# Block sums of weights formed by accumulating transfers instead of VectorE subtractions

## The chip, the cores and the metric

The kernel runs on one core of a Trainium2 chip. Time is device time in microseconds (us) of one execution; the number that counts is the median of several executions. The engines are TensorE (PE for its matmuls, PEld for its weight loads), VectorE (DVE), ScalarE (ACT), GpSimd (POOL) and SyncE (SP). SP issues nearly all transfers between HBM and the on-chip memory (SBUF); POOL can issue transfers too, on a queue of its own, and such a transfer may add what it reads to what already stands at its destination. Matrix products gather in PSUM, which ACT and DVE read.

## The reference

A trunk of two layers, float32, with 512 tokens and a model width of 1024. Each layer is a feed-forward network (FFN), a token mixing of three branches, and a second FFN, each between two norms:

```python
def _swiglu(t, w_gate, w_up, w_down):
    return (jax.nn.silu(t @ w_gate) * (t @ w_up)) @ w_down

for l in range(2):
    f = _swiglu(_rmsnorm(h, ffn1_pre_g[l]), ffn1_w_gate[l], ffn1_w_up[l], ffn1_w_down[l])
    h = h + 0.5 * _rmsnorm(f, ffn1_post_g[l])
    ...            # projections, stick-breaking, forgetting and memory attention, gates, w_out
    f = _swiglu(_rmsnorm(h, ffn2_pre_g[l]), ffn2_w_gate[l], ffn2_w_up[l], ffn2_w_down[l])
    h = h + 0.5 * _rmsnorm(f, ffn2_post_g[l])
```

`w_gate` and `w_up` are 1024 x 2816 each: 22 feature tiles of 128 columns. The change is about the products `t @ w_gate` and `t @ w_up` of twelve of these tiles in each of the four FFNs.

## The kernel before

**Matrix products in three passes.** Every float32 operand is split into a high half, rounded to a shorter format by ACT (L188), and a low half, the difference, by DVE (L189). `mm3` (L212 to L216) then makes three matmuls: high by high, high by low, low by high. A tile of weights is thus loaded (SP), split (ACT, then DVE), and read by PE. The names of the trace follow this: `raw_...` is a loaded tile, `wh_...` and `wl_...` its halves. `us_...` and `ag...` are halves of activations.

**Queue of weights.** Work on weights is a list of jobs (class `Queue`, L372). A job names its units (128x1024 tiles of weights, 512 KB). Ahead of a job, `load_ahead` splits the units of the jobs that come (at least 4 units), and `fetch_ahead` issues their transfers as far as buffers allow. Rings of buffers: two for "raw", four each for "wh" and "wl", six for "v". A scheduler puts the instructions of each engine in an order when the program is built, by estimated times; on the chip each engine works through its own list in that order, and waits where an operand or a buffer isn't there yet.

**Token-major groups.** In each FFN (named a and c for the first and second of a layer; trace names such as `kta`, `pta` or `ktc` leave the numbers out) the feature tiles 14, 16, 18, 20 and 0 are plain pairs, and three groups at f = 2, 6 and 10 (`TG`, L637) cover twelve tiles. A group takes a 2x2 block product, tokens by features, with gate and up side by side, and computes it with seven block products instead of eight, in the order n = 0, 2, 3, 4, 5, 1, 6 (`ORDER`, L640). The weights of a group are four blocks: B00 and B10, the upper and lower half of the rows of `w_gate`, and B01 and B11, the same of `w_up`; each block is two tiles, k0 = 0 and k0 = 2. So a product is a job of two units with 12 matmuls each. The right-hand operand of each product:

| n | weights | formed from |
|---|---|---|
| 0 | B00 | loaded |
| 2 | B01 - B00 | kept, `t` |
| 3 | B11 - B01 + B00 | kept, `t` |
| 4 | B11 | loaded |
| 5 | B11 - B01 | kept, `b` |
| 1 | B10 | loaded |
| 6 | B10 minus the operand of n = 3 | kept, `t` |

The signs of the activation sums (`sums`, L693, on DVE) go with them. `BlockUnit.load` (L328) forms the sums with one DVE subtraction each: L337 for n = 2, L340 for n = 3, L345 for n = 5, L349 for n = 6. They are written in place into two kept tiles per k0, which are of the ring "v" (six buffers, four used by a group). B00 and B10 are loaded a second time for n = 2 and n = 6, B01 and B11 once: 14 loads by SP for a group (L313). After a product, PSUM goes to SBUF by ACT (copies L741, silu L739, L745) or DVE (additions L743); `feature_major` (L751) turns the result.

**What lies around the groups.** The first FFN starts with loads of the input, norms, constants (POOL makes two masks with L144 and L150 in `more_constants`, L139) and small vectors by POOL transfers (`vectors`, L121, turned by PE at L127). In the first group of that FFN stand the statistics of the input `mem` (`mem_stats`, L1057 to L1069): its two 128x1024 tiles (`mst`) are taken from the ring "v" too, ACT squares them (L1062) and changes its function table for Ln and Exp (L1064). At the start of each later FFN, the norm of the four token tiles (L592 to L631: residual and square L601 and L602, normed L608, transposed on PE L618, halves by ACT and DVE) runs beside the last product of the stage before and the first loads of the new weights; `park` (L777) stores the hidden state.

Of the kernel before, what the change touches and what calls it, by code (L numbers as in the profile page):

```python
# [9 lines left out]
F32 = mybir.dt.float32  # L10
F32R = mybir.dt.float32r
BF16 = mybir.dt.bfloat16
AF = mybir.ActivationFunctionType
ALU = mybir.AluOpType
# [3 lines left out]
P = 128  # L18
# [4 lines left out]
def kernel(  # L23
# [38 lines left out]
    nc = tc.nc  # L62
    _, S, D = x.shape
# [3 lines left out]
    ND = D // P  # L67
# [37 lines left out]
    def stile(shape, tag, name, dt=F32R):  # L105
        return sb.tile(shape, dt, tag=tag, bufs=BUFS[tag], name=name)
# [134 lines left out]
    class Unit:  # L241


        def __init__(self, src, k0, nk, c0, ncol, name, scale=None):
            self.tags, self.place = ("wh", "wl"), "raw"
            self.src, self.k0, self.nk, self.c0, self.ncol, self.name, self.scale = src, k0, nk, c0, ncol, name, scale
            self.h = self.raw = None
# [9 lines left out]
        def fetch(self):  # L257
            if not self.waits():
                return
            Q.fetched += self.ring()  # L260
            self.raw = stile([P, self.nk, self.ncol], self.place, "raw_" + self.name, F32)
            nc.sync.dma_start(self.raw[:], self.src[self.k0 * P:(self.k0 + self.nk) * P, self.c0:self.c0 + self.ncol]
                              .rearrange("(k p) c -> p k c", p=P))

        def load(self):
            if self.h is not None:
                return
            self.fetch()
            self.split_from(self.raw[:])
            self.loaded()  # L270
# [17 lines left out]
    class BlockUnit(Unit):  # L288
# [7 lines left out]
        BLOCKS = ((0, 0), (1, 0), (0, 0), None, None, (0, 1), (1, 0))  # L296
# [31 lines left out]
        def load(self):  # L328
            if self.h is not None:
                return  # L330
            self.fetch()
            t = self.keep.get(0, self.k0) if self.n >= 2 else None
            b = self.keep.get(1, self.k0) if self.n >= 3 else None
            if self.n < 2:
                src = self.raw[:]
            elif self.n == 2:
                nc.vector.tensor_tensor(t, t, self.raw[:], ALU.subtract)  # L337
                src = t
            elif self.n == 3:
                nc.vector.tensor_tensor(t, b, t, ALU.subtract)  # L340
                src = t
            elif self.n == 4:
                src = b
            elif self.n == 5:
                nc.vector.tensor_tensor(b, b, self.raw[:], ALU.subtract)  # L345
                src = b
            else:
                ins = (t, self.raw[:]) if self.pair is None else (self.raw[:], t)
                nc.vector.tensor_tensor(t, *ins, ALU.subtract)  # L349
                src = t  # L350
            self.split_from(src)
            if self.ring():
                self.raw = None
                Q.fetched -= 1
            Q.fetch_ahead()
# [125 lines left out]
    Q = Queue()  # L481
# [160 lines left out]
    def ffn(l, src, wg, wu, wd, dst, name, spare, aside=None):  # L642
# [78 lines left out]
        def gate_up(f, n, uns):  # L721
            if n in (0, 1, 2):
                st["gb", SUM[n]] = [pbank("mm", f"pt{name}_{f}_{n}_{e}") for e in range(2)]
            pts = st["gb", SUM[n]]
            opens, ends = n in (0, 1, 2), n in (1, 4, 6)
            for un in uns:
                for k in range(un.nk):
                    kk = un.k0 + k
                    for e in range(2):
                        mm3(pts[e][:], *input_block(n, kk, e), un.h[:, k], un.l[:, k], opens and kk == 0,  # L730
                            ends and kk == ND // 2 - 1, free=True)
                        yield 3 * S * PE_US
            i, j = TO[n]
            if n in (0, 2, 3, 6):
                st["c", i, j] = stile([P, 2, S], "f", f"c{name}_{f}_{i}{j}", F32)
            t = st["c", i, j]
            for e in range(2):
                if n == 6:
                    nc.scalar.activation(t[:, e], pts[e][:], AF.Silu)  # L739
                elif n in (0, 2, 3):  # L740
                    nc.scalar.copy(t[:, e], pts[e][:])  # L741
                else:
                    nc.vector.tensor_tensor(t[:, e], t[:, e], pts[e][:], ALU.add)  # L743
            if n == 1:
                nc.scalar.activation(t[:], t[:], AF.Silu)  # L745
            if n in (1, 6):
                u = st["c", i, 1]
                nc.vector.tensor_tensor(u[:], u[:], t[:], ALU.mult)
                st["hid", f, i] = u

        def feature_major(f):  # L751

            for i in range(2):
                u = st.pop(("hid", f, i))
                for b in range(2):
                    f2 = f + 2 * b
                    pt = pbank("z", f"th{name}_{f2}_{i}")
                    for m in range(2):
                        for e in range(2):
                            nc.tensor.transpose(pt[:, (2 * m + e) * P:(2 * m + e + 1) * P],  # L760
                                                u[:, e, (2 * b + m) * P:(2 * b + m + 1) * P], ident[:])
                    yield 0.45
                    out_ = pt[:].rearrange("p (m q) -> p m q", m=2)
                    nc.scalar.copy(pair(f2)[:, :, HALVES[i]], out_)

        def group(f):

            keep = Keep(lambda i, k0: stile([P, 2, S], "v", f"kt{name}_{f}_{i}_{k0}", F32)[:])
            for n in ORDER:
                uns = []  # L770
                for k in range(0, ND // 2, 2):
                    uns.append(BlockUnit(n, wg[l], ND // 2, k, 2, S, keep, f"t{name}_{f}_{n}_{k}", (wg[l], wu[l])))
                    uns[-1].c0 = f * P
                yield uns, (lambda n=n, uns=uns: gate_up(f, n, uns))
            yield [], lambda: feature_major(f)
# [140 lines left out]
        def turns(f):  # L916
            *jobs, turn = group(f)
            later.append(turn)
            return iter(jobs)
# [774 lines left out]
    for l in LAYERS:  # L1694
        i, mn = 3 * l, []
# [42 lines left out]
```

## Time and profile before

| | |
|---|---|
| median of 3 runs | 2389.71 us (2389.67 to 2389.91) |
| the profiled execution | 2390.63 us, with a span of 2388.9 us |
| busy in the span | PE 2377.2, PEld 2010.7, DVE 1842.9, ACT 1320.8, POOL 74.2 us |
| granted TensorE clock | 0.999 |
| transfers | 334.00 MB, mean 140 GB/s |

The span runs from the first to the last instruction of the profiled execution. Its rows give, for a group of instructions: line, engine, operation, output and inputs with sizes, the count, then busy time, the mean in ns of one, and the idle time just before them with what ended it. A row of the timeline gives the start, the length, the engine and the line; matmuls are pipelined, so their lengths overlap. The view of stretches gives busy us of PE, PEld, DVE, ACT and POOL between two times, then the granted clock, the busy share of the 16 DMA engines, and GB/s. The rows of transfers give the median time from issue to landing.

### The profile page before, as it was taken

Reading aid. Unit: us, or ns where it says so; the run is one execution under the profiler, and the core shown is the slowest. Engines: PE = TensorE matmul, PEld = TensorE weight load, DVE = VectorE, ACT = ScalarE, POOL = GpSimd, SP = SyncE. Lnnn points to the kernel's source line nnn. Section 1 sums busy time; section 2 is a strip of 40 time slices with the busy share of each in tenths; the row PEclk is TensorE's granted clock in tenths of the full one; section 3 lists DMA queues with packets and bytes.
Section 4 is the critical chain, followed back from the end, with each engine's and each line's share of the span. In section 5 each row is a group of like instructions: output and inputs, shape, how many; then the busy total and the mean of one; then the engine's idle time right before and its main releaser. Section 6 shows DMA issues by size and latency. Waiting matters only on the chain.

```text
span 2388.9 us, 30985 instructions
## 1 busy us (share of the span) xinstructions
PE 2377.2 (100%) x11736; PEld 2010.7 (84%) x11736; DVE 1842.9 (77%) x2535; ACT 1320.8 (55%) x2144; POOL 74.2 (3%) x130
## 2 busy tenths in 40 slices
PE   9999999999999999999999999999999999999998
PEld 8888888888888898888898888888888888988887
DVE  7786887677876687769787878876787766778686
ACT  5655455576655555554545554656675655455543
POOL 0000000001110000000000000000001100000000
PEclk9999999999999999999999999999999999999999
DMA  5554554222223445545545546532232244445453
GB/s 188 165 174 136 202 183 143 71 76 77 88 62 116 158 135 174 169 148 195 184 141 166 178 140 220 174 109 80 63 98 71 71 141 142 159 143 183 141 198 129
DMA packets 233979, 334.00 MB, mean 140 GB/s; under 512 B 10315, under 2 KB 133475, under 8 KB 233829
## 3 DMA queue, kind: packets, MB, share of 16 engines
q1 hardware_dynamic: 233728, 331.98, 42.8%
q8 instruction: 92, 1.51, 0.3%
q14 instruction: 59, 0.48, 0.1%
q0 software_dynamic: 96, 0.03, 0.0%
q10 hardware_dynamic: 4, 0.00, 0.0%
HBM read 319.39 MB, written 12.58 MB: 139 GB/s over the span
## 4 chain that ended last, share of the span: by engine, by line
PE 95%; DVE 3%; ACT 1%; DMA 1%; issue 0%; DVEq 0%; ACTq 0%
PE pg L216 3%; PE pg L214 3%; PE pg L215 3%; PE pta L214 3%; PE ptc L216 3%; PE pta L216 3%; PE ptc L215 3%; PE pta L215 3%; PE ptc L214 3%; PE pda L214 3%; PE pda L215 3%; PE pda L216 3%; PE pdc L216 3%; PE pdc L215 3%; PE pdc L214 3%; PE pb L214 2%
## 5 line engine op out<-in xcount | busy, mean ns | idle before, releaser
L214 PE MATMUL pg<-us_a,wh_wg 128*128 128x512 f32 x384 | 150.6, 392 | 0.0
L216 PE MATMUL pg<-us_a,wl_wg 128*128 128x512 f32 x384 | 149.6, 390 | 0.0
L215 PE MATMUL pg<-us_a,wh_wg 128*128 128x512 f32 x384 | 149.5, 389 | 0.0
L188 ACT CAST wh_tc<-ktc 128x1024 fp32r<-128x1024 f32 x60 | 62.6, 1052 | 83.3 <-DVE ktc L349 32.4
L188 ACT CAST wh_ta<-kta 128x1024 fp32r<-128x1024 f32 x60 | 62.6, 1053 | 80.2 <-DVE kta L349 34.1
L189 DVE TENSOR_TENSOR wl_tc<-ktc,wh_tc 128x1024 fp32r<-128x1024 f32 x60 | 72.8, 1223 | 24.4 <-ACT wh_tc L188 24.2
L189 DVE TENSOR_TENSOR wl_ta<-kta,wh_ta 128x1024 fp32r<-128x1024 f32 x60 | 72.9, 1223 | 23.4 <-ACT wh_ta L188 22.9
L216 PE MATMUL pdc<-wh_dc,alc 128*128 128x512 f32 x224 | 87.3, 390 | 0.3 <-DVE alc L189 0.3
L215 PE MATMUL pdc<-wl_dc,ahc 128*128 128x512 f32 x224 | 87.2, 389 | 0.0
L214 PE MATMUL pdc<-wh_dc,ahc 128*128 128x512 f32 x224 | 87.1, 389 | 0.0
L214 PE MATMUL pda<-wh_da,aha 128*128 128x512 f32 x224 | 87.1, 389 | 0.0
L215 PE MATMUL pda<-wl_da,aha 128*128 128x512 f32 x224 | 87.1, 389 | 0.0
L216 PE MATMUL pda<-wh_da,ala 128*128 128x512 f32 x224 | 87.1, 389 | 0.0
L192 DVE SCALAR_TENSOR_TENSOR wl_wg<-raw_wg,wh_wg 128x1024 fp32r<-128x1024 f32 x48 | 58.8, 1224 | 34.0 <-ACT wh_wg L191 29.5
L216 PEld LDWEIGHTS pg<-us_a,wl_wg 128*128 128x128 f32 x384 | 72.1, 188 | 15.2
L215 PEld LDWEIGHTS pg<-us_a,wh_wg 128*128 128x128 f32 x384 | 72.2, 188 | 14.3
L214 PEld LDWEIGHTS pg<-us_a,wh_wg 128*128 128x128 f32 x384 | 72.1, 188 | 14.3
L214 PE MATMUL pta<-wh_ta,aga 128*128 128x512 f32 x192 | 75.2, 391 | 0.0
L214 PE MATMUL ptc<-wh_tc,agc 128*128 128x512 f32 x192 | 75.0, 391 | 0.0
L216 PE MATMUL pta<-wh_ta,aga 128*128 128x512 f32 x192 | 74.7, 389 | 0.0
L216 PE MATMUL ptc<-wh_tc,agc 128*128 128x512 f32 x192 | 74.7, 389 | 0.0
L215 PE MATMUL ptc<-wl_tc,agc 128*128 128x512 f32 x192 | 74.7, 389 | 0.0
(536 smaller groups left out, 7691.3 us busy)
## 6 DMA issues: line engine op xcount, KB each, us to landing
raw_da<-in_ffn_w_down_dram SPq DMA_DIRECT2D x58, 512.0 KB, 3.6
raw_dc<-in_ffn_w_down_dram SPq DMA_DIRECT2D x58, 512.0 KB, 3.4
raw_ta<-in_ffn_w_gate_dram SPq DMA_DIRECT2D x48, 512.0 KB, 3.7
raw_wg<-in_w_gate_dram SPq DMA_DIRECT2D x48, 512.0 KB, 3.5
raw_tc<-in_ffn_w_gate_dram SPq DMA_DIRECT2D x48, 512.0 KB, 3.6
kta<-in_ffn_w_up_dram SPq DMA_DIRECT2D x24, 512.0 KB, 4.9
raw_wo<-in_w_out_dram SPq DMA_DIRECT2D x24, 512.0 KB, 3.3
ktc<-in_ffn_w_up_dram SPq DMA_DIRECT2D x24, 512.0 KB, 5.7
```

The lines of the kernel that those rows point to most:

```text
L188: both = [nc.scalar.copy(h_ap, src)]
L189: make = lambda: nc.vector.tensor_tensor(l_ap, src, h_ap.bitcast(F32), ALU.subtract)
L192: make = lambda: nc.vector.scalar_tensor_tensor(l_ap, src, scale, h_ap.bitcast(F32), ALU.mult, ALU.subtract)
L214: nc.tensor.matmul(pt, lh, rh, start=start, stop=False, skip_group_check=free)
L215: nc.tensor.matmul(pt, lh, rl, start=False, stop=False, skip_group_check=free)
L216: nc.tensor.matmul(pt, ll, rh, start=False, stop=stop, skip_group_check=free)
```

## The change

A new class `SumUnit` takes the place of `BlockUnit` in the groups. It keeps three tiles per k0, so a group holds all six buffers of the ring "v". No sum is formed on DVE any more: ACT writes the negative of a tile into a kept buffer, and a transfer issued by POOL adds another block to it. That block comes from HBM, or in one case from another kept buffer:

| at the load of | before it in the buffer | ACT writes | POOL's transfer adds | then used by |
|---|---|---|---|---|
| n = 0 | | buf0 = -B00 | B01 from HBM | n = 2 |
| n = 0 | buf1: B01, loaded | buf1 = -B01 | B11 from HBM | n = 5 |
| n = 2 | buf2: B00, loaded | | buf1 from SBUF | n = 3 |
| n = 3 | | buf0 = -buf2 | B10 from HBM | n = 6 |

Every row holds for both k0. In a group SP issues 10 loads instead of 14 (three raw blocks and the first contents of buf1 and buf2, each for both k0), POOL issues 8 accumulating transfers, ACT writes 6 negations, and 8 DVE subtractions go. The loads of buf1 and buf2 are issued together with the raw block of n = 0. The order of the products, the matmuls and the splits stay. The new lines move everything behind them down by 71 lines.

```diff
+    class SumUnit(BlockUnit):
+        BLOCKS = ((0, 0), (1, 0), None, None, (1, 1), None, None)
+        def __init__(self, n, src, rows, k0, nk, ncol, keep, name, pair=None, three=True):
+            super().__init__(n, src, rows, k0, nk, ncol, keep, name, pair)
+            self.kept = {2: 0, 3: 2 if three else 1, 5: 1, 6: 0}.get(n)
+            self.three = three
...
+        def plus(self, i, b):
+            if isinstance(b, int):
+                src = self.buf(b)
+            else:
...
+            nc.gpsimd.dma_start(self.buf(i), src, accum_op=ALU.add)
+        def minus(self, i, src):
+            nc.scalar.activation(self.buf(i), src, AF.Copy, scale=-1.0)
+        def fetch(self):
...
+            if self.n == 0:
+                self.block(self.buf(1), (0, 1))
+                if self.three:
+                    self.block(self.buf(2), (0, 0))
+        def load(self):
...
+            self.split_from(self.raw[:] if self.kept is None else self.buf(self.kept))
+            if self.n == 0:
+                self.minus(0, self.raw[:])
+                self.plus(0, (0, 1))
+                self.minus(1, self.buf(1))
+                self.plus(1, (1, 1))
+            elif self.n == 2:
+                if self.three:
+                    self.plus(2, 1)
...
+            elif self.n == 3:
+                self.minus(0, self.buf(self.kept))
+                self.plus(0, (1, 0))
...
-                    uns.append(BlockUnit(n, wg[l], ND // 2, k, 2, S, keep, f"t{name}_{f}_{n}_{k}", (wg[l], wu[l])))
+                    uns.append(SumUnit(n, wg[l], ND // 2, k, 2, S, keep, f"t{name}_{f}_{n}_{k}", (wg[l], wu[l])))
```

`three` is true wherever the class is used; its other branch, with two kept tiles, isn't reached.

More of the change, by code (lines that the diff above doesn't have):

```diff
@@ L351, in load, with buf @@
             self.split_from(src)
+            if self.ring():
+                self.raw = None
+                Q.fetched -= 1
+            Q.fetch_ahead()
+    class SumUnit(BlockUnit):
[4 more added lines that the diff above has]
+            self.three = three
+        def buf(self, i):
+            return self.keep.get(i, self.k0)
+        def plus(self, i, b):
+            if isinstance(b, int):
+                src = self.buf(b)
+            else:
+                r = (b[0] * self.rows + self.k0) * P
+                src, c = (self.src, b[1] * self.ncol) if self.pair is None else (self.pair[b[1]], self.c0)
+                src = src[r:r + self.nk * P, c:c + self.ncol].rearrange("(k p) c -> p k c", p=P)
+            nc.gpsimd.dma_start(self.buf(i), src, accum_op=ALU.add)
+        def minus(self, i, src):
+            nc.scalar.activation(self.buf(i), src, AF.Copy, scale=-1.0)
+        def fetch(self):
+            if self.fetched:
+                return
+            self.fetched = True
+            if self.ring():
+                Q.fetched += 1
+                self.raw = stile([P, self.nk, self.ncol], "raw", "raw_" + self.name, F32)
+                self.block(self.raw[:], self.BLOCKS[self.n])
+            if self.n == 0:
[3 more added lines that the diff above has]
+        def load(self):
+            if self.h is not None:
+                return
+            self.fetch()
+            self.split_from(self.raw[:] if self.kept is None else self.buf(self.kept))
[7 more added lines that the diff above has]
+                    self.plus(2, 1)
+                else:
+                    self.plus(1, (0, 0))
+            elif self.n == 3:
+                self.minus(0, self.buf(self.kept))
+                self.plus(0, (1, 0))
+                if not self.three:
+                    self.block(self.buf(1), (0, 1))
+            elif self.n == 4 and not self.three:
+                self.minus(1, self.buf(1))
+                self.plus(1, (1, 1))
```

## The prediction

> **What bounds the kernel now.** I read the page first, then the waits of PE, then stretches of the three token-major groups.
>
> ```profile
> span 2388.9 us, 30985 instructions
> PE 2377.2 (100%) x11736; PEld 2010.7 (84%) x11736; DVE 1842.9 (77%) x2535; ACT 1320.8 (55%) x2144; POOL 74.2 (3%) x130
> PEclk9999999999999999999999999999999999999999
> PE 95%; DVE 3%; ACT 1%; DMA 1%; issue 0%; DVEq 0%; ACTq 0%
> ```
>
> ```profile
> PE warm L1608 <- DVE warm L1692: 1.3, 1, 1.3
> PE ptf L1176 <- DVE pf L1247: 0.7, 2, 0.4
> ...
> PE pga L803 <- ACT w_ga L188: 0.2, 1, 0.2
> ```
>
> ```profile
> 60.00:98.60 38.60, 38.60 (x170) 31.65 (x170) 28.22 (x37) 24.31 (x34) 0.00 (x0) 1.00 0.49 159
> 98.60:138.50 39.90, 39.90 (x186) 33.25 (x186) 33.55 (x32) 21.60 (x28) 0.00 (x0) 1.00 0.57 187
> 902.00:1022.60 120.60, 120.60 (x551) 100.34 (x550) 98.16 (x96) 64.59 (x81) 0.00 (x0) 1.00 0.52 164
> ```
>
> The chain that ended last is 95% TensorE, at full clock. PE's whole list of waits has seven rows, the longest 1.3 us. The stretches (columns: PE, PEld, DVE, ACT, POOL, clock, DMA share, GB/s) are the first two groups of layer 0's first FFN and all three of its second: PE is busy in every one from end to end, DVE 71 to 84%, ACT 54 to 63%. So what the change takes from DVE is beside PE's work. The question is which weight half it makes late.
>
> **What is removed and added.** Rows by shape, then transfers with their median time to landing, then two rows of POOL:
>
> ```profile
> L345 DVE TENSOR_TENSOR kta<-kta,raw_ta 128x1024 f32<-128x1024 f32 x12 | 14.5, 1223 | 0.3
> L188 ACT CAST wh_ta<-kta 128x1024 fp32r<-128x1024 f32 x60 | 62.6, 1053 | 80.2 <-DVE kta L349 34.1 <-PE pua L215 15.7 <-DVE kta L340 9.0
> L189 DVE TENSOR_TENSOR wl_ta<-kta,wh_ta 128x1024 fp32r<-128x1024 f32 x60 | 72.9, 1223 | 23.4 <-ACT wh_ta L188 22.9
> L741 ACT COPY ca<-pta 128x512 f32<-128x512 f32 x36 | 20.4, 583 | 5.5 <-PE pta L216 5.5
> L1062 ACT ACTIVATE mst<-mst 128x1024 f32<-128x1024 f32 x2 | 2.1, 1061 | 0.1
> L1064 ACT ACT_TABLE_LOAD x1 | 1.3, 1283 | 0.0
> ```
>
> ```profile
> raw_ta<-in_ffn_w_gate_dram SPq DMA_DIRECT2D x48, 512.0 KB, 3.7
> ktc<-in_ffn_w_up_dram SPq DMA_DIRECT2D x24, 512.0 KB, 5.7
> kta<-in_ffn_w_up_dram SPq DMA_DIRECT2D x24, 512.0 KB, 4.9
> mst<-in_mem_dram SPq DMA_DIRECT2D x2, 512.0 KB, 6.2
> vecs<-in_b_gate_dram POOLq DMA_DIRECT2D x1, 24.0 KB, 2.1
> ```
>
> ```profile
> 27.80 1.15 POOL L144 TENSOR_SCALAR_AFFINE_SELECT c<-c 128x128 f32<-128x128 f32 x1 [19.73 <-DVE c L143]
> 35.73 0.56 POOL L124 DMA_DIRECT2D vecs<-in_b_gate_dram  x1
> ```
>
> Twelve groups run (three in each of four FFNs), of two units each. A unit loses 4 subtractions on DVE: 96 x 1.22 = 117 us, which buys nothing where PE is full; I count 0. ACT gains 3 negations a unit, 72 x 1.05 = 76 us, 6.3 us a group on top of 21.6: room enough, if none of them waits. SP issues 10 loads a group instead of 14. POOL issues 8 accumulating transfers a group, at 0.56 us each from the L124 row (4.5 us of 39.9).
>
> No row shows an accumulating transfer. Let L be its time from issue to landing. Not less than a plain load, 3.7; not more than two of the slowest kind, 2 x 5.7 = 11.4. A POOL transfer of 24 KB takes 2.1, 512 KB add 3.7 - 2.1 = 1.6 for each stream, and kta loads that land behind others take 1.2 more than raw_ta: 2.1 + 2 x 1.6 + 1.2 = 6.5 if source and destination are both read. I take 6.5, nearest to the POOL row, and keep both ends.
>
> The Trainium skill (DMA: Bandwidth & Descriptors, Anatomy of one DMA) fits 2.0 us plus bytes over 436 GB/s for such a transfer; with two reads that is an estimate of 4.4 us, and the sum below would be 2.5 us smaller. No row here shows it.
>
> **Steady groups: 0.** The tightest chain leads from one group's fifth job to the next group's second. The load of the second B01 waits for the buffer that job n=5 reads, ACT negates it, POOL accumulates (L), waits for the landing because the next entry of its queue reads that sum, and behind it stands the accumulation for job n=2 (L again). In the second FFN:
>
> ```profile
> 916.62 1.06 ACT L188 CAST wh_tc<-ktc 128x1024 fp32r<-128x1024 f32 x1 [1.19 <-issue]
> ```
>
> ```profile
> 946.30 0.39 PE L214 MATMUL ptc<-wh_tc,agc 128*128 128x512 f32 x1
> ```
>
> 916.6 + 1.05 + 1.22 (split) + 5.7 (load) + 1.05 (negation) = 925.6; two POOL issues 1.1, and 2 L: 926.7 + 2L. PE wants the first half of n=2 at 946.3, so its split must begin by 943.9: L may be 8.6. At 6.5 there are 4 us to spare, and I take 0; at 11.4 each of the 8 later groups would lose 2 x 2.8 = 5.6 us. DMA engines: 14 transfers now take 57% of 39.9 us, 1.62 each; 10 plain and 8 accumulating ones take 29 us if these cost the same, 42 if double, which is more than the 39.9 there are.
>
> **First group of the first FFN: +5.7.** This is the only one with other work in it: statistics of mem (L1062 to L1069), whose two tiles share the ring of six "v" buffers. Now a group holds four, and the mst loads went out at 57.9 us (the first of the rows below; the others are times of DVE and PE that the next two paragraphs use). Afterwards a group holds all six, so the first mst load waits for the buffer of the n=3 sum, the second for its twin. In the built order of ACT the two squares stand among the splits, with four table loads (two before): split n4/k0, square, copy, table load, Ln, square, table load, Exp, split n4/k1, table load, Ln, copy, table load, Exp, split n5/k0.
>
> ```profile
> 57.94 0.89 SPq L1061 DMA_DIRECT2D mst<-in_mem_dram  x2
> ```
>
> ```profile
> 34.75 2.35 DVE L189 TENSOR_TENSOR wl_ga<-raw_ga,wh_ga 128x1024 fp32r<-128x1024 f32 x2
> 40.64 1.22 DVE L189 TENSOR_TENSOR wl_ua<-raw_ua,wh_ua 128x1024 fp32r<-128x1024 f32 x1
> ```
>
> ```profile
> 68.44 0.39 PE L214 MATMUL pta<-wh_ta,aga 128*128 128x512 f32 x1
> ...
> 79.61 0.39 PE L214 MATMUL pta<-wh_ta,aga 128*128 128x512 f32 x1
> ...
> 82.33 0.39 PE L214 MATMUL pta<-wh_ta,aga 128*128 128x512 f32 x1
> ```
>
> The chain: on DVE the low half of ua_14 now stands behind five activation sums and halves, about 46.6 instead of 41.9 done; its raw buffer takes the first block, landed 51; split and negation to 53.1; accumulation lands 59.7; then split, low half, negation, split of k1 (64.2), its low half (65.4), negation (66.5), split n3/k0 and low half to 68.8. Only now does the mst load start: 75.1 at 6.2 us. On ACT from there: square 1.2, copy 0.6, table 1.3, Ln 0.2, square 1.2, table 1.3, Exp 0.2: 81.1; split n4/k1 and its low half: 83.4. PE wants it at 79.8 (its second matmul): 3.6 us late. Then two table loads, copy, two small ones: 85.9, split and low half of n5/k0 88.2; PE, shifted, wants it at 86.1: 2.1 more. Bounds: with a 3.7 us load and L = 3.7 it shrinks by 5.3 to 0.4; with L = 11.4 it grows by 4.9 to 10.6. Behind it the chain to the next group starts late: +0.5 (0 to 2).
>
> **Starts of the FFNs: +1.7.** In the first, two things on POOL's queue come to stand behind accumulations that wait for landings: the mask (L144) and the transfers of vecs (L123, L124).
>
> ```profile
> 38.40 0.39 PE L216 MATMUL pga<-us_x,wl_ga 128*128 128x512 f32 x1
> ...
> 59.81 0.22 PE L127 MATMUL vecs_t<-ident,vecs 8*128 8x8 f32 x1
> ```
>
> DVE waits for the mask, and the low halves of ga_14 come after it: the first of the pair is done at 34.75 + 1.18 = 35.9, PE wants it at 38.4, so 2.4 us of delay cost nothing: +0.5 (0 to 3). The second vecs transfer goes at about 55.9 by the chain above and lands 2.1 later at 58.0; PE turns vecs at 59.8: 0, within the same bounds. On SP's queue the kept blocks now go ahead of the stores of the hidden state and the first weight loads of a later FFN: two loads of 3.7 us, asked for while the norm is still running, with PE on the last product of the stage before: 0. In the third FFN, a negation whose load has just left stands on ACT ahead of the square that the norm of token tile 2 waits for:
>
> ```profile
> 1202.03 1.06 ACT L558 ACTIVATE fc<-hc 128x1024 f32<-128x1024 f32 x1 [0.47 <-DVE hc L601]
> ```
>
> ```profile
> 1205.30 1.28 DVE L608 SCALAR_TENSOR_TENSOR fc<-hc,nhc,gqc 128x1024 f32<-128x1024 f32 x1
> ```
>
> ```profile
> 1206.92 1.03 PE L618 MATMUL utc<-ident,fc 128*128 128x128 f32 x8
> ```
>
> fc is ready at 1206.6 and PE takes it at 1206.9. ACT was free for 0.47 us before the square, so 1.05 us pushes it by 0.6 at least: 0.3 late, 1.3 if the load lands a us later: +0.8. In the second and fourth FFN two negations stand there, but tile 3's norm has 1.6 us to spare:
>
> ```profile
> 865.21 1.28 DVE L608 SCALAR_TENSOR_TENSOR fb<-hm,nhb,gqb 128x1024 f32<-128x1024 f32 x1
> ```
>
> ```profile
> 868.09 0.60 PE L618 MATMUL utb<-ident,fb 128*128 128x128 f32 x4
> ```
>
> Ready at 866.5, transposed at 868.1: +0.2 each, 0 to 1.
>
> Sum: 5.7 + 0.5 + 0.5 + 0.8 + 0.4 = 7.9 us. The profiled execution took 2390.6, so 2398.5; it stands 0.9 above the median of the runs, 2389.7, so I forecast 2397.6 (+0.33%). 0.2% (4.8 us) is about what a measurement here tells from no change.
>
> **Rivals.** *Hidden* (2388.5 to 2394.5): the mst loads land sooner or the scheduler's waits overlap better; the sum at the low bounds is 0.4 + 0 + 0 + 0.3 + 0 = 0.7. For it: the tightest low half of a group is that of n2/k1, behind the subtractions, and that squeeze goes:
>
> ```profile
> 105.04 1.22 DVE L189 TENSOR_TENSOR wl_ta<-kta,wh_ta 128x1024 fp32r<-128x1024 f32 x1
> ```
>
> ```profile
> 107.03 0.39 PE L215 MATMUL pta<-wl_ta,aga 128*128 128x512 f32 x1
> ```
>
> It is done at 106.3 and wanted at 107.0.
>
> *The transfers bound the groups* (2449): at L = 11.4 the sum is 10.6 + 2 + 3 + 1.3 + 2 + 8 x 5.6 = 64, less some 5 where these overlap. For it: 42 us of DMA in 39.9; against it: time of packets is not yet throughput, and a group that is late also asks later. The Trainium skill says that a reducing transfer runs at half the rate of a copying one, since its two reads go through one ring (Collectives: The Full Stack, The bandwidth ceiling); by that rule this rival's 42 us hold. No trace shows such a transfer yet.
>
> *Faster* (below 2385): DVE's relief would have to end waits of PE. Place: the low halves of n2/k1. Price: at most what PE waits there, and PE shows no idle time in these stretches; it decides only if such waits hide inside matmuls, 0.5 us in each of 12 groups. Nearly excluded.
>
> **How the numbers follow.** Forecast 50%, transfers bound 25%, hidden 22%, faster 3%. So faster 0.03, same 0.22, slower 0.75. The forecast's own range is 2394.5 to 2406. The 8-in-10 range leaves out the lower half of hidden and the top of the transfers: 2390 to 2445.
>
> **What the new profile would show.** Landing of kta accumulations near 6.5 us; PE waits on wl_ta around 80 to 90 us, nearly 6 us in all, behind ACT's table loads L1064 and L1065, four of them; a wait of some tenths at L618 near 1207; no PE wait in the second to twelfth group beyond 1 us; DVE down by 117 us, ACT up by 76. Wrong if the accumulations land after 8.6 us (PE waits in every group), or if the mst squares come before 73 us.

## The result and the profile after

The changed kernel takes 2458.48 us (median of 4 runs, 2456.38 to 2459.77), the kernel before 2389.69 beside it: ratio 1.0288, 95% interval 1.0275 to 1.0300. That is 68.8 us more. The forecast was 2397.6 and the range ended at 2445; the case that came nearest was the rival "the transfers bound the groups" with 2449.

The page of the changed kernel (busy time, transfer queues, times to landing):

```profile
span 2458.1 us, 31131 instructions
PE 2405.0 (98%) x11736; PEld 2024.8 (82%) x11736; DVE 1731.1 (70%) x2439; ACT 1389.2 (57%) x2218; POOL 181.1 (7%) x226
q1 hardware_dynamic: 220672, 306.81, 38.1%
q0 software_dynamic: 23136, 50.37, 12.1%
kta<-in_ffn_w_up_dram POOLq DMA_DIRECT2D x24, 512.0 KB, 8.1
ktc<-in_ffn_w_up_dram POOLq DMA_DIRECT2D x24, 512.0 KB, 7.6
kta<-kta POOLq DMA_DIRECT2D x12, 512.0 KB, 6.9
kta<-in_ffn_w_gate_dram POOLq DMA_DIRECT2D x12, 512.0 KB, 5.8
```

VectorE lost 111.8 us and ScalarE gained 68.4 (forecast: 117 and 76). TensorE does the same 11736 matmuls, but is busy 27.8 us longer (2405.0 against 2377.2) and idle 41.4 us longer (span less busy: 53.1 against 11.7); the two make the 69.2 us that the span grew. The idle time, from the waits of TensorE:

```profile
PE pta L214 <- ACT ca L810: 15.8, 8, 3.5
PE ptc L214 <- ACT cc L810: 13.9, 7, 3.7
PE vecs_t L128 <- DMA vecs<-in_b_gate_dram: 3.6, 1, 3.6
PE vecs_t L127 <- DMA vecs<-in_mem_norm_g_dram: 2.8, 1, 2.8
PE pta L215 <- DVE wl_ta L189: 1.7, 5, 0.7
PE pga L216 <- DVE wl_ga L189: 1.4, 1, 1.4
```

The first two rows are new, and each has a place: the start of product n = 2 in the second and third group of every FFN. Both kernels make the same matmuls in the same order but for two, so the start of each can be set against its start before. The delay grows by 8.8 and 7.7 us at these places in the first FFN, 6.7 and 7.4 in the second, 4.8 and 7.7 in the third, 4.3 and 8.2 in the fourth: 56 us in eight groups, 6.9 each. The start of the first FFN and its first group lose 13.2, the start of the third FFN 0.8. TensorE is released by L810, a silu on ScalarE; it stands behind the split of the n = 2 sum, which waits for a landing.

One such place, the second group of the second FFN, in the timelines of POOL, ACT and PE:

```profile
956.30 1.19 POOL L382 DMA_DIRECT2D ktc<-in_ffn_w_up_dram  x1 [2.90 <-ACT ktc L385]
965.73 0.91 POOL L382 DMA_DIRECT2D ktc<-ktc  x1 [8.24 <-DVE cc L814]
966.30 2.80 POOL L382 DMA_DIRECT2D ktc<-in_ffn_w_up_dram  x2
```

```profile
954.95 1.06 ACT L385 ACTIVATE ktc<-ktc 128x1024 f32<-128x1024 f32 x1 [2.38 <-DMA ktc<-in_ffn_w_up_dram]
...
965.08 1.06 ACT L385 ACTIVATE ktc<-raw_tc 128x1024 f32<-128x1024 f32 x1 [1.57 <-DMA raw_tc<-in_ffn_w_gate_dram]
...
975.59 1.05 ACT L188 CAST wh_tc<-ktc 128x1024 fp32r<-128x1024 f32 x1 [7.55 <-DMA ktc<-in_ffn_w_up_dram]
976.54 0.59 ACT L810 ACTIVATE cc<-ptc 128x512 f32<-128x512 f32 x1
```

```profile
977.18 0.50 PE L214 MATMUL ptc<-wh_tc,agc 128*128 128x512 f32 x1 [1.22 <-ACT cc L810]
```

The accumulation into the second buf1 goes at 956.3. The next entry of the queue reads that sum and goes at 965.7. (Its row names an instruction of DVE that ended about then; the entry waits for several events, the landing among them.) Behind it the two accumulations for n = 2 go at 966.3 and 967.0, and the split of the first starts at 975.6. Their times to landing, each from a window that holds one of them alone, in the order of their issue, and last one that goes alone later, at 979.3:

```profile
ktc<-in_ffn_w_up_dram POOLq DMA_DIRECT2D x1, 512.0 KB, 8.4
ktc<-ktc POOLq DMA_DIRECT2D x1, 512.0 KB, 6.7
ktc<-in_ffn_w_up_dram POOLq DMA_DIRECT2D x1, 512.0 KB, 9.2
ktc<-in_ffn_w_up_dram POOLq DMA_DIRECT2D x1, 512.0 KB, 12.0
ktc<-in_ffn_w_gate_dram POOLq DMA_DIRECT2D x1, 512.0 KB, 5.9
```

The first lands 1.0 us before the next entry goes. The three behind it are in flight together and land at 972.5, 975.5 and 979.0, some 3 us apart. This is the chain that the prediction laid out. From the first issue to the landing of the first half of n = 2 it takes 19.2 us, where the prediction tolerated 18.3 (2 x 8.6 and two issues) and reckoned with 14.1. The prediction has no term for the second half of n = 2, which lands 3.5 us later still. In all eight places TensorE waits 1.5 to 3.0 us for it. The two accumulations for n = 2 take 8.7 to 10.8 and 11.0 to 12.7 us there; the one into buf1 before them takes 5.8 to 6.3 in five of the eight, and 7.6, 8.4 and 9.9 in the others. The transfer engines in that time, and as they were before with plain loads alone (the share of the DMA engines and GB/s are the last two columns):

```profile
951.00:963.00 12.00, 12.00 (x55) 9.94 (x54) 6.75 (x9) 6.55 (x7) 2.08 (x2) 1.00 1.05 295
967.00:975.00 8.00, 8.00 (x37) 6.64 (x36) 2.36 (x2) 1.04 (x2) 2.10 (x2) 1.00 1.06 220
```

```profile
938.00:946.00 8.00, 8.00 (x37) 6.64 (x36) 6.76 (x6) 3.80 (x5) 0.00 (x0) 1.00 1.01 369
```

With the engines full, plain loads alone move 369 GB/s; with accumulations among them it is 295 and 220 GB/s in these stretches.

Over the whole transition TensorE is no longer busy from end to end, at a mean clock of 0.95:

```profile
943.00:983.00 40.00, 36.48 (x154) 29.28 (x153) 19.60 (x20) 22.33 (x27) 7.97 (x8) 0.95 0.84 206
```

### The profile page after: what moved, and what is told of

Same layout as the page of the kernel before. It is cut to its first block, busy times and chain, and to the rows that moved or that the text cites. A ratio compares the mean times of both kernels' runs of the same rounds, so it can differ in the third digit from the quotient of the medians.

```text
span 2458.1 us, 31131 instructions
## 1 busy us (share of the span) xinstructions
PE 2405.0 (98%) x11736; PEld 2024.8 (82%) x11736; DVE 1731.1 (70%) x2439; ACT 1389.2 (57%) x2218; POOL 181.1 (7%) x226
## 3 DMA queue, kind: packets, MB, share of 16 engines
q0 software_dynamic: 23136, 50.37, 12.1%
## 5 line engine op out<-in xcount | busy, mean ns | idle before, releaser
L189 DVE TENSOR_TENSOR wl_ta<-kta,wh_ta 128x1024 fp32r<-128x1024 f32 x48 | 58.8, 1224 | 83.5 <-ACT wh_ta L188 83.4
L189 DVE TENSOR_TENSOR wl_tc<-ktc,wh_tc 128x1024 fp32r<-128x1024 f32 x48 | 58.7, 1224 | 75.0 <-ACT wh_tc L188 75.0
L214 PE MATMUL pta<-wh_ta,aga 128*128 128x512 f32 x192 | 80.0, 416 | 16.6 <-ACT ca L810 15.8
L214 PE MATMUL ptc<-wh_tc,agc 128*128 128x512 f32 x192 | 79.9, 416 | 13.9 <-ACT cc L810 13.9
L215 PE MATMUL pta<-wl_ta,aga 128*128 128x512 f32 x192 | 78.7, 410 | 1.1 <-DVE wl_ta L189 1.1
L188 ACT CAST wh_ta<-kta 128x1024 fp32r<-128x1024 f32 x48 | 50.4, 1050 | 50.9 <-DMA kta<-in_ffn_w_up_dram 32.7
L188 ACT CAST wh_tc<-ktc 128x1024 fp32r<-128x1024 f32 x48 | 50.5, 1052 | 49.8 <-DMA ktc<-in_ffn_w_up_dram 29.1
L216 PE MATMUL pta<-wh_ta,aga 128*128 128x512 f32 x192 | 78.0, 406 | 0.0
```

The lines of the kernel that those rows point to most:

```text
L188: both = [nc.scalar.copy(h_ap, src)]
L189: make = lambda: nc.vector.tensor_tensor(l_ap, src, h_ap.bitcast(F32), ALU.subtract)
L214: nc.tensor.matmul(pt, lh, rh, start=start, stop=False, skip_group_check=free)
L215: nc.tensor.matmul(pt, lh, rl, start=False, stop=False, skip_group_check=free)
L216: nc.tensor.matmul(pt, ll, rh, start=False, stop=stop, skip_group_check=free)
```

## The experiments

Three theories stood against each other. *Queue* or *order*: an entry that waits for a landing stands ahead of something that is due sooner, and another order would hide the long landings. *Throughput*: an accumulating transfer takes the transfer engines twice as long, so landings are long wherever they stand. *ScalarE*: the negations come too late. A table first; "units" counts the transfers of a new-style group in plain loads of 512 KB, an accumulating one as two. A unit takes 1.62 us of all engines, so a group of 39.9 us has room for 24.6.

| kernel | units in a group | median us | ratio to before, 95% |
|---|---|---|---|
| before | 14 | 2389.7 | 1 |
| only the n = 5 sum accumulated | 14 + 4 | 2393.2 | 1.0015 (1.0006 to 1.0025) |
| plain transfers in place of accumulating | 10 + 8 | 2393.3 | 1.0018 (1.0009 to 1.0028) |
| half-size accumulations | 10 + 8 | 2400.2 | 1.0045 (1.0030 to 1.0060) |
| before, with extra plain transfers | 14 + 6 | 2405.6 | 1.0064 (1.0047 to 1.0081) |
| before, with extra accumulations | 14 + 12 | 2441.9 | 1.0216 (1.0201 to 1.0232) |
| the change | 10 + 16 | 2458.5 | 1.0288 (1.0275 to 1.0300) |
| the change, GpSimd's order | 10 + 16 | 2462.0 | 1.0301 (1.0285 to 1.0316) |
| the change, program's order | 10 + 16 | 2470.6 | 1.0338 (1.0321 to 1.0356) |
| the change, n = 3 sum on VectorE | 10 + 12 | 2470.4 | 1.0344 (1.0329 to 1.0359) |
| the change, two kept tiles | 10 + 20 | 2489.2 | 1.0417 (1.0402 to 1.0433) |

**Another order on GpSimd's queue.**

```diff
-                self.minus(0, self.raw[:])
-                self.plus(0, (0, 1))
                 self.minus(1, self.buf(1))
                 self.plus(1, (1, 1))
+                self.minus(0, self.raw[:])
+                self.plus(0, (0, 1))
...
-            nc.gpsimd.dma_start(self.buf(i), src, accum_op=ALU.add)
+            tc.keep_in_program_order(nc.gpsimd.dma_start(self.buf(i), src, accum_op=ALU.add))
```

> The changed kernel with one thing moved: on GpSimd's queue, both accumulations that start from ScalarE's negatives (into buf1, then into buf0) stand ahead of the accumulation buf2 += buf1, which waits for a landing. All work is kept. Theory queue (job n=2's sum comes late because it stands behind a queue entry that waits for a landing): the later groups lose under 1 us each instead of 6.9, the time is 2400 to 2410. Theory throughput (the transfer engines are full, because an accumulating transfer costs them twice, whatever its place): 2445 to 2460. Theory ScalarE (the negation of the raw block, and the split behind it, come too late): 2440 to 2460 too, with the waits moved to products n=2 and n=3.

Measured 2462.0, 2 us above the range of the other two theories: the queue theory falls. The entry that waited is out of the way, but four accumulations are now in flight together, and the wait turns up on ScalarE: its built order puts the negation of buf2 ahead of the second split of n = 2. The timelines of POOL, ACT and PE of this kernel:

```profile
962.70 1.40 POOL L382 DMA_DIRECT2D ktc<-ktc  x1
```

```profile
974.92 1.06 ACT L385 ACTIVATE ktc<-ktc 128x1024 f32<-128x1024 f32 x1 [7.19 <-DMA ktc<-ktc]
```

```profile
977.46 0.50 PE L214 MATMUL ptc<-wh_tc,agc 128*128 128x512 f32 x1 [3.56 <-ACT cc L810]
```

The transfer from buf1 to buf2 goes at 962.7 and is awaited until 974.9, 12.2 us, and TensorE waits 3.6 us at the same place as before.

**The n = 3 sum on VectorE.**

```diff
-                    self.plus(2, 1)
+                    nc.vector.tensor_tensor(self.buf(2), self.buf(2), self.buf(1), ALU.add)
```

> The changed kernel, but buf2 += buf1 is done by VectorE (24 additions of 1.22 us) and not by a transfer; six accumulating transfers a group stay. Theory queue: no entry of GpSimd's queue waits for a landing any more, so the later groups lose under 1 us each: 2398 to 2408. Theory throughput: a quarter of the accumulated bytes goes, so a quarter to a third of the 55 us of the later groups: 2440 to 2445. Theory ScalarE: about 2455.

Measured 2470.4, more than any theory gave, and with less to transfer. The addition waits on VectorE for buf1's landing, and VectorE's queue holds what TensorE needs at once: additions that empty PSUM (L814), low halves, and at the FFNs' starts the norm (L679). The waits of TensorE and one such addition:

```profile
PE ptc L214 <- DVE cc L814: 12.1, 4, 3.5
PE pta L214 <- DVE ca L814: 10.0, 4, 3.0
PE utb L689 <- DVE fb L679: 6.7, 2, 4.7
```

```profile
961.22 1.23 DVE L412 TENSOR_TENSOR ktc<-ktc,ktc 128x1024 f32<-128x1024 f32 x1 [3.88 <-DMA ktc<-in_ffn_w_up_dram]
```

So the place of a wait does matter, for the worse: this run shows what a landing costs when it is awaited on a busier queue. It also shows that the count of units alone does not set the loss: 22 units fit into the 24.6 that there is room for, the engines are at 0.67 between 918 and 990 us, and the loss is larger than with 26.

**Plain transfers in place of the accumulating ones.**

```diff
-            nc.gpsimd.dma_start(self.buf(i), src, accum_op=ALU.add)
+            nc.gpsimd.dma_start(self.buf(i), src)
```

> The changed kernel with plain transfers in place of the accumulating ones: same issues, queue, sizes, waits, but the addition is left out (what lands replaces what stood there). Theory throughput and theory queue both expect landings near 4 to 5 us instead of 8 and the later groups to lose under 1 us each: 2393 to 2403, the rest being the first group of the first FFN. Theory ScalarE: no more than 20 us better than the changed kernel, 2440 to 2455. If landings stay above 7 us, it is GpSimd's queue and not the addition that makes them long.

Measured 2393.3. With the same queue, order, negations and waits, the loss is down from 68.8 to 3.5 us. Its page:

```profile
q0 software_dynamic: 13920, 50.37, 6.2%
kta<-in_ffn_w_up_dram POOLq DMA_DIRECT2D x24, 512.0 KB, 5.4
kta<-kta POOLq DMA_DIRECT2D x12, 512.0 KB, 3.7
```

The same 50.37 MB take 6.2% of the engines' span instead of 12.1%: 0.062 x 2391.3 / 96 = 1.54 us a transfer against 0.121 x 2458.1 / 96 = 3.10. An accumulating transfer takes the engines as long as two plain ones. The size of the packets is not the reason: accumulations from HBM come in packets of 2 KB, which take 192 ns in the mean, against 97 for SP's plain packets of that size. ScalarE's 72 negations are all still there, so that theory falls too.

**Half-size accumulations.**

```diff
-            nc.gpsimd.dma_start(self.buf(i), src, accum_op=ALU.add)
+            nc.gpsimd.dma_start(self.buf(i)[:, 0], src[:, 0], accum_op=ALU.add)
```

> The changed kernel, but each accumulating transfer adds only the first of the two 128-row parts of its tile (256 KB instead of 512); the second part of each sum is left out. All waits and orders stay, and the transfer engines get 10 + 8 units a group instead of 10 + 16. Theory throughput: the stalls go with the saturation, 2393 to 2405, as with plain transfers. Theory that accumulation as such is late (a fixed delay of the add, of its issue by GpSimd, or of the chain of waits): half or more of the loss stays, 2425 or more.

Measured 2400.2: accumulation as such is not late. Landings are at 3.7 to 5.2 us in the medians, and two larger losses are left, in the first FFN (6.2 us at 59 to 69 us, where the small vectors are awaited, and 4.4 at 110 to 117). In this run and the one before, the landings are shorter and the engines have room, both at once; the next pair takes the two apart.

**The traffic alone, beside the kernel before, and its control.**

```diff
+            if self.n == 0 and self.pair is not None:
+                nc.gpsimd.memset(self.keep.get(9, self.k0), 0.0)
...
+            if self.pair is not None and self.n in (0, 3):
+                for b_ in ((0, 1), (1, 1)) if self.n == 0 else ((1, 0),):
...
+                    nc.gpsimd.dma_start(self.keep.get(9, self.k0), ..., accum_op=ALU.add)
```

> The kernel before, with its sums on VectorE, and beside them six accumulating transfers a group from HBM into two spare buffers of the ring v that nobody reads (cleared by GpSimd once a group). The transfer engines get as much as in the changed kernel, counting an accumulating transfer double: 14 + 12 against 10 + 16 a group. Left out: nothing; the extra sums are not used. Theory order, and any theory by which only the waiting for the sums costs: 2390 to 2396. Theory throughput (the groups are bound by the transfers): 2420 or more.

The control leaves out `accum_op`:

> The control to the extra traffic beside the kernel before: the same extra transfers into the same two spare buffers, but plain ones, which the transfer engines do in half the time (14 + 6 units a group against 14 + 12). Theory throughput (the doubled time of an accumulating transfer on the engines is what costs): 2390 to 2400. If the other things that came with the extra traffic cost (six buffers of the ring v in use, GpSimd clearing them): 2425 or more, near the 2442 of the accumulating ones.

Measured 2441.9 and 2405.6. The control missed its 2400: six more plain transfers a group, two more buffers in use and GpSimd's clearing cost 15.9 us together; no run takes these apart. The 36.3 us between the two come with `accum_op` alone, in a kernel in which nobody reads the sums. Of these, 5.5 stand at 38 to 47 us, at the low halves of ga_14 behind GpSimd's mask, which goes 3 us later than in the control. Accumulations slow the plain loads beside them: the raw blocks of `w_up` land after 6.7 us in the median, against 5.8 and 6.0 in the control. The engines' share in the accumulating one over two groups:

```profile
918.00:990.00 72.00, 68.97 (x312) 56.80 (x311) 55.07 (x51) 34.70 (x43) 13.22 (x12) 1.00 0.87 229
```

**Negations, splits and accumulations in the program's order.** GpSimd's edit as in the first experiment, and:

```diff
-            nc.scalar.activation(self.buf(i), src, AF.Copy, scale=-1.0)
+            tc.keep_in_program_order(nc.scalar.activation(self.buf(i), src, AF.Copy, scale=-1.0))
...
+            was, Q.pinned = Q.pinned, True
             self.split_from(self.raw[:] if self.kept is None else self.buf(self.kept))
+            Q.pinned = was
```

> The changed kernel with GpSimd's accumulations, ScalarE's negations and the splits (ScalarE and VectorE) of the groups held in the order in which the program names them: buf1's accumulation, buf0's, buf2's, and on ScalarE no negation that waits for buf2 ahead of the split of n=2. All work is kept. Theory order (long landings alone would be hidden, but an entry that waits for a landing stands on some engine ahead of work that is due sooner): the later groups lose under 1 us each, the first FFN's first group about 10, so 2400 to 2405. Theory throughput (the transfer engines can't deliver the sums of a group in time in any order): 2440 or more.

Measured 2470.6. The order theory falls a second time: accumulations from `w_up` take 11.2 us in the median of the first FFNs and 11.0 in that of the second ones, and every later group still stalls.

**One sum a group by accumulation.** The kernel before, where `c` holds B01, and its n = 5 no longer subtracts:

```diff
+                    nc.scalar.activation(c, c, AF.Copy, scale=-1.0)
...
+                    nc.gpsimd.dma_start(c, ..., accum_op=ALU.add)
```

> The kernel before with only the sum of n = 5 formed by ScalarE's negative and an accumulating transfer (two of these a group, in a third kept buffer, 14 plain loads as before: 14 + 4 units a group); the other three sums stay on VectorE. Theory throughput: 18 units of 1.62 us are 29 us of a group's 39.9, so the engines are not full and it costs under 3 us: 2388 to 2393. Any theory by which one accumulating transfer in the chain is too slow: above 2400.

Measured 2393.2, 0.2 above the expected range. Two accumulations a group are all but hidden; they gain nothing either.

**Two kept tiles.**

```diff
-        def __init__(self, n, src, rows, k0, nk, ncol, keep, name, pair=None, three=True):
+        def __init__(self, n, src, rows, k0, nk, ncol, keep, name, pair=None, three=False):
```

> The changed kernel with the other branch of its class: two kept tiles per k0, sums formed by five accumulating transfers and five plain loads per k0, so 10 + 20 units a group instead of 10 + 16; no transfer from one kept buffer to another, all ten come from HBM. Theory throughput: 30 units of 1.62 us are 48.6 us against the group's 39.9, about 8.7 us more than there is in each of the eight later groups, and more than the changed kernel by 6.5 us in each: 2480 to 2520. Theory chain (what costs is the accumulation from a buffer that itself waits for one, and its place in the queue): that one is gone, 2400 to 2440.

Measured 2489.2, as throughput has it: with 30 units for 24.6, the loss is 99.4 us. No transfer reads another kept buffer here, but the run doesn't rule the chain out: buf1 takes two accumulations in a row, and GpSimd's queue still waits for the landing of the first (3.8 us before the entry at 986.5).

**First groups alone, later groups alone.**

```diff
-                    uns.append(SumUnit(n, ...
+                    uns.append((SumUnit if f == 2 else BlockUnit)(n, ...
```

> The new sums only in the first group (f = 2) of each FFN; the groups at f = 6 and 10 form theirs on VectorE as before. By the gaps of TensorE in the trace of the changed kernel: about 2.0 + 5.6 + 1.2 + 0.9 us in the first FFN, 0.7 in the third, so 2400 (2397 to 2403). If the loss of the later groups were made by the first ones before them, it would be more, up to 2430.

> The new sums only in the groups at f = 6 and 10; the first group of each FFN (f = 2) forms its sums on VectorE as before. If the losses of first and later groups simply add: 2390 + (2458 - 2402) = 2446 (2438 to 2452). If the later groups lose only because a first group with accumulating transfers goes ahead of them: 2415 to 2430.

Measured 2402.5 and 2453.1. The first groups lose 12.7 us, within the range. The later ones lose 63.4 on their own, above the range: together that is 76, and the change loses 68.8, so they don't simply add, but the later groups don't need the first ones to lose.

**The small vectors out of the way.** In the kernel with new sums in the first groups, the use of the vectors comes after the first group:

```diff
             Q.add([], vectors)
...
+        some(7)
+        if name == "a0":
+            Q.add([], vectors)
```

> The kernel with the new sums only in the first groups (2402.5), and in it TensorE's use of the small vectors (L127, L128), whose transfers stand between accumulations on GpSimd's queue, moved behind the first group of the first FFN. If those transfers are the main cost there: the stall of 4.2 us at 66 us and 1.2 us of half clock go, 2397 (2396 to 2398.5). If the accumulations for n = 2 are late all the same and stand next in line (ready about 68.3 and 72.2 us, wanted then at 67.6 and 70.3): a stall of some 2.5 us takes its place, 2399 to 2401. If GpSimd's queue has nothing to do with it: 2402 to 2403.

Measured 2405.5 (2401.4 to 2406.4), nothing gained; all three expectations missed. The waits and ScalarE's timeline say what came in its place:

```profile
PE pta L214 <- ACT ca L812: 7.8, 2, 6.0
```

```profile
81.16 1.06 ACT L1134 ACTIVATE mst<-mst 128x1024 f32<-128x1024 f32 x1 [4.29 <-DMA mst<-in_mem_dram]
...
86.76 1.03 ACT L188 CAST wh_ta<-raw_ta 128x1024 fp32r<-128x1024 f32 x1
87.80 1.28 ACT L1136 ACT_TABLE_LOAD   x1
...
89.21 0.57 ACT L812 COPY ca<-pta 128x512 f32<-128x512 f32 x1
```

The late mst load, then table loads, then the copy that TensorE waits for: 6.0 us at once. This is the stall of the prediction's first group. In the changed kernel the wait for the vectors comes first and makes TensorE late, and 0.9 us of this stall is left, at 89 us.

## Why the prediction was wrong

- **The step that failed: one L = 6.5 for every accumulation, and with it "steady groups: 0".** The chain was the right one, and 6.5 is near the 5.8 to 6.3 us that buf1's last accumulation took in five of the eight places. It fails for the two accumulations for n = 2, which go within 2 us of each other right behind buf2's: 8.7 to 10.8 us and 11.0 to 12.7. The sum for L was made from a transfer that has the engines to itself, a 1.6 us stream twice; the 1.2 us for "behind others" was too little for three accumulations together with the raw loads, at shares above 1. The limit of 8.6 was worked out for the first half of n = 2 alone, with the chain starting 20.2 us before TensorE wants that half (926.1 to 946.3). It started 15.7 to 19.7 us before, in the six places with a stall of over 0.9 us there, and the second half lands later still. Eight groups lost 56 us instead of 0.
- **The rival that took place.** "The transfers bound the groups" gave 2449 at L = 11.4. Its count, 42 us of transfers in 39.9, holds: 10 x 1.62 + 8 x 3.10 = 41.0. It got a quarter of the chances, and the range cut off its top. That it came near is luck in part: it counted one late chain (5.6 us a group, measured 6.9), and knew nothing of the half clock. The mean does not bind either: over whole later groups, 42.6 to 47.3 us long (four of the eight), the engines' share is 0.84 to 0.91. What I didn't work out is that the transfers aren't spread over the group: those for the next products come together at its end, where the engines are full (share 1.05).
- **The rule that spoke against the change.** The Trainium skill (Collectives: The Full Stack, The bandwidth ceiling) gives the reducing step of a collective half the rate of the copying one, because it has two sources to read. By the engines' share it is 3.10 against 1.54 us for the transfers here: the trace agrees on the ratio. The estimate by the fit of the Trainium skill (DMA: Bandwidth & Descriptors, Anatomy of one DMA), 4.4 us, lies below every landing of an accumulation in the changed kernel, 5.0 to 12.7 us.
- **A term that no case had: half the clock.** After the stalls TensorE runs slower for some us (below). Of the 69.2 us, 27.8 are longer busy time, and matmuls at the lower rate lose 20.4.
- **First group of the first FFN: +5.7 forecast.** The place lost 13.2 with its start, but most of it not there: 2.0 at the low halves of ga_14 behind GpSimd's mask (forecast 0.5, 0 to 3), and 9.3 at the small vectors, which were forecast at 0 (waits of 2.8 and 3.6 us, then half clock). Their second transfer went at 61.1 us and not at 55.9, since the accumulations ahead landed later, and these few KB took 6.7 and 7.5 us to land themselves, where 2.1 was reckoned:

```profile
vecs<-in_mem_norm_g_dram POOLq DMA_DIRECT2D x1, 4.0 KB, 6.7
vecs<-in_b_gate_dram POOLq DMA_DIRECT2D x1, 24.0 KB, 7.5
```

- **The mst stall.** It cost 0.9, as the delay by the vectors covers it; without that delay, 6.0 of it came out. Another 1.0 us stands at 109 us, at a low half.
- **Starts.** Third FFN: 0.8 against +0.8, right. Second and fourth: nothing seen against +0.2 each.
- **Costs at nothing.** VectorE's 112 us bought nothing: right; every run with the new sums took longer than before. GpSimd's issue is 1.19 us and not 0.56 for the transfers from HBM. (In the stretches that the prediction shows, VectorE is busy 73 to 84%, not 71 to 84; nothing hangs on it.)

What stays open: whether an order exists in which the 26 units of a group are hidden after all. Two were tried and neither helped; the wait moved to another queue each time. It is also open how the loss divides between long landings and loads that are slowed beside them. Only the extra traffic, whose sums nobody awaits, shows the second without the first: 36.3 us more than its control.

## What to carry to other kernels

A transfer that adds at its destination costs the transfer engines two plain ones, so count it twice in the budget of the stretch in which it must land, not in the mean of the kernel: 18 units in a group cost 0.2 to 0.5% here, 26 cost 2.9%. Count also how many such transfers are in flight at once: alone they landed in under 6 us here, as the last of three in 11 to 13. The budget is not all: with 22 units and the wait on VectorE's queue the loss was 3.4%. Moving work off an engine that had slack to a resource that had less was a loss here, and a landing that is late held up what stood behind it on the queue that waited for it. And an experiment that takes one wait away should be read by what waits next.

## What was not expected of the hardware

The clock of TensorE falls to half after stalls of a few us, and comes back late. Stretches of the changed kernel (PEclk is the column before the last two), and two matmuls of the second stretch:

```profile
121.00:124.40 3.40, 1.17 (x3) 0.38 (x3) 1.07 (x2) 1.55 (x3) 0.00 (x0) 0.68 0.24 48
124.40:129.00 4.60, 4.55 (x11) 3.59 (x12) 3.43 (x4) 4.60 (x6) 2.44 (x2) 0.50 0.31 48
129.00:133.00 4.00, 4.00 (x26) 3.48 (x25) 2.13 (x2) 1.08 (x2) 0.00 (x0) 1.00 1.09 209
```

```profile
125.89 0.63 PE L214 MATMUL pta<-wh_ta,aga 128*128 128x512 f32 x1
126.32 0.63 PE L215 MATMUL pta<-wl_ta,aga 128*128 128x512 f32 x1
```

A stall of 3.6 and one of 2.2 us stand here, with three matmuls between. The clock is at 0.50 from 122.2 to 129.0, in the second stall and for 4.4 us behind it, with matmuls 0.43 us apart instead of 0.227; then it is back at 1.00. The changed kernel has nine such stretches, of 3.4, 6.8 or 10.2 us, and its matmuls lose 1.6 to 2.9 us in each, 20.4 us in all. Stalls of 1.4 and 2.2 us, at 977 and 981 us, were enough; so was one of 2.0 us with only stalls under 0.6 us before it, at 1336 us. It doesn't follow every such stall: not a single one of 1.6 us at 40 us, and not 1.4 and 2.0 us at 968 and 970 us in the kernel before with extra accumulations. So a stall that brought the clock down cost itself and some 2 us more; which stalls do, these traces don't settle. The Trainium skill (TensorE: Matmul & The Clock Gate, What's actually happening) says that an idle window of about 3.4 us halves the clock, and as long a busy one restores it. The lengths of the nine stretches agree, being one, two or three times 3.4 us; the stalls need not be that long, as the 2.0 us at 1336 us show.
